# Hybrid encoder on one core: the output projection's weight sums paced by the local strips, and a v strip at the end of chunk 2

## The chip, the core and the metric

The kernel runs on one core of one Trainium2 chip. The metric is device time in microseconds (us) of one execution. Five engines work side by side: TensorE (PE in the profile, its weight loads PEld), VectorE (DVE), ScalarE (ACT), GpSimd (POOL) and SyncE (SP), which here issues every DMA. Each engine has its own instruction stream, worked through in order; semaphores tie the streams together. Sixteen DMA engines carry the transfers.

## The reference

One encoder layer is applied to a prompt of 1024 tokens and to a sample of 256 tokens, each with 16 meta tokens in front, model width 2048, float32:

```python
u = rms_norm(h, norm_w) @ w_in
qa, ka, va, za, qb, kb, vb, zb = jnp.split(u, split_points(), axis=-1)
qa = rope(rms_norm(qa, q_norm_a)); ka = rope(rms_norm(ka, k_norm_a))
ya = global_gqa(qa, ka, va) * jax.nn.silu(za)             # 8 heads, 2 key/value heads
qb = rms_norm(qb, q_norm_b); kb = rms_norm(kb, k_norm_b)
yb = neighbourhood_attention(qb, kb, vb, rpb) * jax.nn.silu(zb)  # 8 heads, windows of 8 x 16
y = jnp.concatenate([ya, yb], axis=-1) @ w_out
return h + y
```

A head is 128 wide. The input projection has 52 column strips of 128: for the global heads 8 q, 2 k, 2 v and 8 z, for the local heads 8 each of q, k, v and z.

## The kernel before

**Precision.** A float32 product is made of three matmuls in a reduced format. Each operand is split into a high part (a cast on ScalarE) and the remainder (a subtraction on VectorE); `split`, L48, does both.

**Two chunks.** Tokens are worked in two chunks: `chunk1` (L456) has the meta tokens, the sample and 384 prompt tokens (656 columns), `chunk2` (L564) the other 640. In each chunk x is loaded tile by tile into the pool `xr` (four buffers, L962), scaled, split and kept for the whole chunk (`get_x`, L72). Then the strips follow.

**A strip.** `strips` (L104) multiplies one 128-wide column strip of `w_in` with the chunk's tokens: sixteen 128 x 128 tiles in four pieces of 256 KB, 96 matmuls into two PSUM tiles of pool `pp` (four buffers). The pieces are loaded into `raw` and split into `w` (four buffers each), traced at a higher priority (`woff`) so that they run ahead. In chunk 1 the low part is also stored to `wld`, and chunk 2 loads it back. `project` (L424) calls `strips` and then evacuates: q and k with an RMS norm (`qk_evac`, L136; a partition sum on GpSimd, for global heads the rope with four small DMAs `ts` per block), v with a product and transposes on TensorE (`v_rows`, `v_turn`), z with a silu made of Abs, Exp, Ln and Exp on ScalarE (`z_evac`, L176). The first `project` call of a chunk does two strips together (k and v), as does the last one of chunk 1 (v and z).

**Order of strips.** Chunk 1 runs 20 global strips (k, v, and per head z and q, each head followed by a small attention over two key tiles, `attend`) and then 32 local strips (k, q, v, z per head, each head followed by `attend_sample`). Chunk 2 runs the global strips with four attention blocks per head. Its local strips are in the list `late` (L713); eight of them are put between the global heads (`fill`), the others alternate with blocks of the local attention of heads 0 to 6 (`local_blocks`, L703). `v_local` (L604) stores v to `vn`, and `v_windows` loads the windows from there; `z_late` stores z to `zd`, and `z_load` loads it. The four blocks of the last local head run among the first eight products of the output projection.

**Weight sums.** The output projection (`outproj`, L869) uses seven products of half-size blocks instead of eight, which needs differences of the blocks of `w_out`. `w_sums` (L434) makes them ahead of time: a generator of sixteen steps, and a step loads four pieces of 256 KB into `xr` (tile `wq`), does four subtractions on VectorE (L439) and stores four pieces to `td`. `project` advances it at every second strip once more than 8 have been traced.

**Output projection.** At its start the PSUM pool `pp` is closed and `pq` opens in its place; the y halves (`yr`, in the buffers of `xr`) are loaded, combined and split into `ym`, which lies where chunk 2's x was. `products` (L815) does 48 matmuls a step.

**What sets the order.** The kernel's text gives a priority by order of tracing. A scheduler simulates the machine as the program is built and, for each engine, takes the ready instruction that was traced first; an instruction that is ready early runs early, unless a buffer, a dependence or an explicit order holds it back. `issue_after(i)` gives such an order: what is traced in it on i's engine is queued behind i, without a wait for i's end.

Of the kernel before, what the change touches and what calls it, by code (L numbers as in the profile page):

```python
# [12 lines left out]
F32 = mybir.dt.float32  # L13
F32R = mybir.dt.float32r
AF = mybir.ActivationFunctionType
ALU = mybir.AluOpType
# [24 lines left out]
QA, KA, VA, ZA, QB_, KB, VB, ZB = 0, 8, 10, 12, 20, 28, 36, 44  # L41


class Kern:
# [3 lines left out]
    def split(self, hi, lo, full):  # L48
        nc = self.nc
        nc.scalar.copy(hi, full)  # L50
        nc.vector.tensor_tensor(out=lo, in0=full, in1=hi.bitcast(F32), op=ALU.subtract)  # L51

    def rsqrt(self, ms, n):

# [49 lines left out]
    def strips(self, jobs, getx):  # L104


        nc, tc = self.nc, self.tc
        out = [[pool.tile([P, 512], F32, tag=tag, name="pp") for pool, tag in pools] for _, _, pools in jobs]
        for c in range(KT // WCH):
            ws = []  # L110
            for s, _, _ in jobs:
                with tc.high_priority(offset=self.woff):
                    w = self.raw.tile([P, WCH, P], F32, tag="raw", name="wr")
                    self.lastw = nc.sync.dma_start(w[:], self.io["w_in"][s][:, c * WCH:(c + 1) * WCH, :]).ins
                    wh = self.w.tile([P, WCH, P], F32R, tag="wh", name="wh")
                    wl = self.w.tile([P, WCH, P], F32R, tag="wl", name="wl")
                    if self.second:
                        nc.sync.dma_start(wl[:].bitcast(F32), self.wld[s][:, c * WCH:(c + 1) * WCH, :])
                        nc.scalar.copy(wh[:], w[:])  # L119
                    else:  # L120
                        self.split(wh[:], wl[:], w[:])
                ws.append((wh, wl))
                if not self.second:
                    nc.sync.dma_start(self.wld[s][:, c * WCH:(c + 1) * WCH, :], wl[:].bitcast(F32))
            for k in range(WCH):
                kt = c * WCH + k
                xh, xl = getx(kt)
                for (wh, wl), ps, (_, blocks, _) in zip(ws, out, jobs):
                    for p, (o, n) in zip(ps, blocks):
                        first, last = kt == 0, kt == KT - 1  # L130
                        nc.tensor.matmul(p[:, :n], wh[:, k, :], xh[:, o:o + n], start=first, stop=False)  # L131
                        nc.tensor.matmul(p[:, :n], wh[:, k, :], xl[:, o:o + n], start=False, stop=False)  # L132
                        nc.tensor.matmul(p[:, :n], wl[:, k, :], xh[:, o:o + n], start=False, stop=last)  # L133
        return out
# [289 lines left out]
    def project(self, *parts):  # L424

        if not self.second:
            self.projected += len(parts)
            if self.projected > 8 and self.projected % 2 == 0:
                next(self.sums, None)
        jobs = [(p[0], p[1], [p[3] if len(p) > 3 else (self.pp, "pp")] * len(p[1])) for p in parts]  # L430
        out = self.strips(jobs, self.get_x)
        return [p[2](ps) for p, ps in zip(parts, out)]

    def w_sums(self):  # L434

        nc, w = self.nc, self.io["w_out"]

        def sub(out, a, b):
            nc.vector.tensor_tensor(out=out, in0=a, in1=b, op=ALU.subtract)  # L439

        for s in range(8):
            for i in range(0, 8, WCH):
                q = {}
                for n, c, j in (("12", 8 + s, i), ("11", s, i), ("22", 8 + s, 8 + i), ("21", s, 8 + i)):
                    r = self.xr.tile([P, WCH, P], F32, tag="xr", name="wq")
                    nc.sync.dma_start(r[:], w[c][:, j:j + WCH, :])
                    q[n] = r[:]
                sub(q["11"], q["12"], q["11"])
                sub(q["12"], q["22"], q["12"])
                sub(q["22"], q["22"], q["11"])  # L450
                sub(q["21"], q["22"], q["21"])
                for n, p in (("11", 5), ("12", 7), ("22", 6), ("21", 4)):
                    nc.sync.dma_start(self.td[s][p][:, i:i + WCH, :], q[n])
                yield
# [109 lines left out]
    def chunk2(self):  # L564
        nc, io = self.nc, self.io
# [38 lines left out]
        def v_local(s, h):  # L604

            def evac(ps):
                for p, (o, n) in zip(ps, BL):
                    j, e = 3 + o // P, 3 + (o + n) // P
                    vt = self.ev.tile([P, n // P, P], F32, tag="ev", name="vl")
                    nc.scalar.copy(vt[:], self.v_turn(self.v_rows(p, o, n), range(0, n, P)))  # L610
                    nc.sync.dma_start(self.vn[h][P * j:P * e].rearrange("(t p) d -> p t d", p=P), vt[:])
            return s, BL, evac
# [12 lines left out]
        def q_strip(s, h, wc, rope):  # L625
            q = self.q.tile([P, 2, NP], F32R, tag="q", name="q")
            nc.sync.dma_start(q[:, :, :C1P].bitcast(F32), self.qd[h][:])

            def evac(ps):
                for p, (o, n) in zip(ps, BL):  # L630
                    rp = (ct[:, o:o + n], st[:, o:o + n]) if rope else None
                    self.qk_evac(p, o, n, wc, rp, [(0, n, q[:, 0, C1P + o:C1P + o + n], q[:, 1, C1P + o:C1P + o + n])])
                return q
            return s, BL, evac
# [12 lines left out]
        def qk_late(s, wc, dst):  # L647
            def evac(ps):
                for p, (o, n) in zip(ps, BL):
                    self.qk_evac(p, o, n, wc, None, [(0, n, dst[:, o:o + n], None)])  # L650
            return s, BL, evac

        def z_late(s, dst):
            def evac(ps):
                for p, (o, n) in zip(ps, BL):
                    zt = self.ev.tile([P, n], F32, tag="ev", name="zt")
                    self.z_evac(p, o, n, [(0, n, zt[:])])
                    nc.sync.dma_start(dst[:, C1P + o:C1P + o + n], zt[:])
            return s, BL, evac
# [53 lines left out]
        late = []  # L713
        for h in range(NH):
            late += [qk_late(KB + h, kwb, self.k2d[2 + h]), qk_late(QB_ + h, qwb, self.q2d[8 + h]),
                     v_local(VB + h, h), z_late(ZB + h, self.zd[8 + h])]

        def fill(n):
            for _ in range(min(n, len(late))):
# [2 lines left out]
        for g in range(2):  # L722
# [5 lines left out]
            for h in range(4 * g, 4 * g + 4):  # L728
                z, = pr(z_strip(ZA + h, h) + (((self.sp, "sp"),) if h == 0 else ()))
                q, = pr(q_strip(QA + h, h, qw, True))  # L730
# [327 lines left out]
```

## Time and profile before

| | |
|---|---|
| median of 3 runs | 2307.06 us (2305.71 to 2307.85) |
| the profiled execution | 2303.17 us, span 2301.4 us |
| PE, PEld busy | 2233.8 us (97%), 2218.7 us (96%) |
| DVE, ACT, POOL busy | 1594.2 us (69%), 1145.0 us (50%), 525.1 us (23%) |
| DMA | 424.54 MB, mean 184 GB/s |
| loads `wq` and stores `td` | 64 each, 256 KB, 5.9 and 4.4 us to landing (median) |
| mean granted clock of TensorE | 0.991 |

The page is of one execution. Times in the trace count from the span's start. A group's row has the line, the engine, the operation, output and inputs by the program's names, the shape and the count, then busy time, the mean of one in ns, and the engine's idle time before the instructions with what ended it. Rows of waits read: who waited, for what, us in total, how often, the longest. "SPq" is SP's queue issuing a DMA.

### The profile page before, as it was taken

To read this page: it belongs to the slowest core of one execution; us is meant where nothing else is said; L and a number is where in the kernel's file an instruction comes from. 1 tells how busy PE (TensorE), PEld (TensorE's weight loads), DVE (VectorE), ACT (ScalarE), POOL (GpSimd) and SP (SyncE) were. 2 spreads that over 40 slices of the span, in tenths; PEclk is the share of its full clock that TensorE was granted. 3 is DMA by queue.
4 is the path that set the end of the run, shared out by engine and by line. 5 is a ranking of instruction groups with operands and counts; after the bars stand their busy time and mean duration, and the time that the engine had idled before them with its cause. 6 is when DMAs were issued, how large, how long until landed. Compare 5 with 4: busy or idle time off the path is not lost.

```text
span 2301.4 us, 42253 instructions
## 1 busy us (share of the span) xinstructions
PE 2233.8 (97%) x15550; PEld 2218.7 (96%) x15550; DVE 1594.2 (69%) x2988; ACT 1145.0 (50%) x2432; POOL 525.1 (23%) x275
## 2 busy tenths in 40 slices
PE   7988999999999999999999999999999989999999
PEld 6888889999999999999999999999999989999999
DVE  5787578555555565999988999887665667545753
ACT  5444345444344456677767667655444454232220
POOL 0232033112212112342323322333333222000000
PEclk9999999999999999999999999999999999999999
DMA  7888886555555567444544444477777764755663
GB/s 237 258 273 258 283 268 191 179 168 173 175 172 173 172 205 214 120 125 133 135 137 130 128 130 125 150 206 221 212 207 214 209 194 115 231 177 171 184 206 116
DMA packets 279856, 424.54 MB, mean 184 GB/s; under 512 B 48576, under 2 KB 121184, under 8 KB 279648
## 3 DMA queue, kind: packets, MB, share of 16 engines
q1 hardware_dynamic: 279648, 421.84, 60.6%
q8 instruction: 122, 2.00, 0.4%
q14 instruction: 86, 0.70, 0.1%
HBM read 296.25 MB, written 118.90 MB: 180 GB/s over the span
## 4 chain that ended last, share of the span: by engine, by line
PE 79%; DMA 11%; DVE 5%; ACT 2%; SPq 2%; issue 1%; POOL 1%; DVEq 0%; POOLq 0%; ACTq 0%
PE pp L132 17%; PE pp L133 16%; PE pp L131 16%; PE pq L826 5%; PE pq L825 5%; PE pq L824 5%; DMA wq<-in_w_out 3%; DMA xr<-in_x 2%; DMA td<-wq 1%; PE sp L253 1%; PE po L295 1%; PE po L294 1%; PE po L293 1%; PE sp L254 1%; PE sp L255 1%
## 5 line engine op out<-in xcount | busy, mean ns | idle before, releaser
L131 PE MATMUL pp<-xh,wh 128*128 128x384 f32 (+2 forms) x3328 | 1030.6, 313 | 21.7 <-ACT xh L81 17.5
L132 PE MATMUL pp<-xl,wh 128*128 128x384 f32 (+2 forms) x3328 | 1037.1, 312 | 0.5 <-DVE xl L82 0.2
L133 PE MATMUL pp<-xh,wl 128*128 128x384 f32 (+2 forms) x3328 | 1037.6, 312 | 0.0
L131 PEld LDWEIGHTS pp<-xh,wh 128*128 128x128 f32 x3328 | 628.5, 190 | 24.8 <-ACT xh L81 19.8
L132 PEld LDWEIGHTS pp<-xl,wh 128*128 128x128 f32 x3328 | 630.7, 190 | 2.1 <-DVE xl L82 2.1
L133 PEld LDWEIGHTS pp<-xh,wl 128*128 128x128 f32 x3328 | 630.8, 190 | 0.1
L51 DVE TENSOR_TENSOR wl<-wr,wh 128x512 fp32r<-128x512 f32 x320 | 238.7, 759 | 155.1 <-ACT wh L50 130.5
L141 POOL PARTITION_ALL_REDUCE m<-ms x104 | 234.5, 2254 | 410.7 <-ACT ms L139 304.0
L824 PE MATMUL pq<-ym,wh 128*128 128x320 f32 x896 | 277.7, 310 | 8.9 <-DVE z L179 8.9
L826 PE MATMUL pq<-ym,wl 128*128 128x320 f32 x896 | 277.9, 310 | 0.0
L825 PE MATMUL pq<-ym,wh 128*128 128x320 f32 x896 | 277.6, 310 | 0.0
L50 ACT CAST wh<-wr 128x512 fp32r<-128x512 f32 x320 | 193.2, 617 | 161.6 <-PE pp L132 104.0
L222 POOL PARTITION_ALL_REDUCE tot<-a x80 | 170.2, 2128 | 437.2 <-DVE a L220 425.7
L205 POOL PARTITION_ALL_REDUCE ma<-m x80 | 113.4, 1418 | 494.5 <-DVE m L203 494.5
L824 PEld LDWEIGHTS pq<-ym,wh 128*128 128x128 f32 x896 | 169.0, 189 | 9.1 <-ACT ym L50 9.1
L825 PEld LDWEIGHTS pq<-ym,wh 128*128 128x128 f32 x896 | 169.0, 189 | 0.0
L826 PEld LDWEIGHTS pq<-ym,wl 128*128 128x128 f32 x896 | 169.0, 189 | 0.0
L119 ACT CAST wh<-wr 128x512 fp32r<-128x512 f32 x208 | 127.7, 615 | 55.2 <-PE pp L132 52.6
L57 ACT ACTIVATE rs_l<-m 128x384 f32<-128x384 f32 (+2 forms) x104 | 49.1, 472 | 141.1 <-DVE m L142 141.0
L51 DVE TENSOR_TENSOR pl<-S,ph 128x512 fp32r<-128x512 f32 x136 | 95.9, 711 | 7.9 <-ACT ph L50 7.8
L257 ACT COPY S<-sp 128x512 f32<-128x512 f32 x136 | 78.1, 580 | 45.6 <-PE sp L255 38.5
L274 ACT ACTIVATE S<-S 128x512 f32<-128x512 f32 x136 | 83.9, 629 | 32.0 <-DVE S L273 31.8
(200 smaller groups left out, 3396.2 us busy)
## 6 DMA issues: line engine op xcount, KB each, us to landing
wr<-in_w_in SPq DMA_DIRECT2D x416, 256.0 KB, 3.7
wld<-wl SPq DMA_DIRECT2D x208, 256.0 KB, 3.8
wl<-wld SPq DMA_DIRECT2D x208, 256.0 KB, 3.4
yr<-yd SPq DMA_DIRECT2D x72, 320.0 KB, 4.0
wq<-in_w_out SPq DMA_DIRECT2D x64, 256.0 KB, 5.9
td<-wq SPq DMA_DIRECT2D x64, 256.0 KB, 4.4
wr<-td SPq DMA_DIRECT2D x64, 256.0 KB, 3.5
wr<-in_w_out SPq DMA_DIRECT2D x48, 256.0 KB, 4.0
```

Source lines behind the costliest of these rows:

```text
L50: nc.scalar.copy(hi, full)
L51: nc.vector.tensor_tensor(out=lo, in0=full, in1=hi.bitcast(F32), op=ALU.subtract)
L119: nc.scalar.copy(wh[:], w[:])
L131: nc.tensor.matmul(p[:, :n], wh[:, k, :], xh[:, o:o + n], start=first, stop=False)
L132: nc.tensor.matmul(p[:, :n], wh[:, k, :], xl[:, o:o + n], start=False, stop=False)
L133: nc.tensor.matmul(p[:, :n], wl[:, k, :], xh[:, o:o + n], start=False, stop=last)
L141: nc.gpsimd.partition_all_reduce(m2[:], ms[:], P, RED.add)
L205: nc.gpsimd.partition_all_reduce(ma[:], m1[:], P, RED.max)
L222: nc.gpsimd.partition_all_reduce(tot[:], a1[:], P, RED.add)
L824: nc.tensor.matmul(ps[:, b, :B], wh, yh[:, o], start=k == 0, stop=False)
L825: nc.tensor.matmul(ps[:, b, :B], wh, yl[:, o], start=False, stop=False)
L826: nc.tensor.matmul(ps[:, b, :B], wl, yh[:, o], start=False, stop=k == 7)
```

## The change

`w_sums` now yields twice a step: after its four loads, and after the subtractions and stores. The subtractions are put behind the last weight split traced so far, which `split` now returns and `strips` keeps as `lastsplit`. `project` advances the generator at each call once more than 18 strips have been traced: the first loads are traced at strip 19, the first subtractions at strip 20, the last ones at strip 50. In chunk 2, each local head's z strip is now ahead of its v strip, so the last strip before the output projection is a v strip.

```diff
@@ split
-        nc.vector.tensor_tensor(out=lo, in0=full, in1=hi.bitcast(F32), op=ALU.subtract)
+        return nc.vector.tensor_tensor(out=lo, in0=full, in1=hi.bitcast(F32), op=ALU.subtract).ins
@@ strips
-                        self.split(wh[:], wl[:], w[:])
+                        self.lastsplit = self.split(wh[:], wl[:], w[:])
@@ project
-            if self.projected > 8 and self.projected % 2 == 0:
+            if self.projected > 18:
                 next(self.sums, None)
@@ w_sums
                     q[n] = r[:]
-                sub(q["11"], q["12"], q["11"])
-                sub(q["12"], q["22"], q["12"])
-                sub(q["22"], q["22"], q["11"])
-                sub(q["21"], q["22"], q["21"])
+                yield
+
+                with self.tc.issue_after(self.lastsplit):
+                    sub(q["11"], q["12"], q["11"])
+                    sub(q["12"], q["22"], q["12"])
+                    sub(q["22"], q["22"], q["11"])
+                    sub(q["21"], q["22"], q["21"])
                 for n, p in (("11", 5), ("12", 7), ("22", 6), ("21", 4)):
                     nc.sync.dma_start(self.td[s][p][:, i:i + WCH, :], q[n])
                 yield
@@ chunk2
-                     v_local(VB + h, h), z_late(ZB + h, self.zd[8 + h])]
+                     z_late(ZB + h, self.zd[8 + h]), v_local(VB + h, h)]
```

## The prediction

> **What bounds the kernel now.** I first read the forty slices of the page and the lines of its chain.
>
> ```profile
> PE   7988999999999999999999999999999989999999
> ...
> DMA  7888886555555567444544444477777764755663
> ...
> PE pp L132 17%; PE pp L133 16%; PE pp L131 16%; PE pq L826 5%; PE pq L825 5%; PE pq L824 5%; DMA wq<-in_w_out 3%; DMA xr<-in_x 2%; DMA td<-wq 1%; PE sp L253 1%; PE po L295 1%; PE po L294 1%; PE po L293 1%; PE sp L254 1%; PE sp L255 1%
> ```
>
> TensorE is the bound nearly everywhere. It is short of full in the first slices (57.5 us each) and in slice 33, and the first six slices are also the ones where the DMA engines are fullest. The chain names two transfers of the weight sums, the loads `wq` and the stores `td`. So I asked when the sums run.
>
> ```profile
> L446 SPq DMA_DIRECT2D wq<-in_w_out x64: 328/424/1242, 49.2 to 330.8; - x64
> L439 DVE TENSOR_TENSOR wq<-wq x64: 669/692/1630, 55.4 to 337.2; 128x512 f32<-128x512 f32 x64
> L453 SPq DMA_DIRECT2D td<-wq x64: 319/327/726, 56.1 to 343.5; - x64
> ...
> DMA to landing us min/median/max: 2.0/5.2/8.6
> ```
>
> All sixteen steps run between 49 and 344 us, though the text traces them over strips 10 to 40: nothing but a free `xr` buffer holds their loads back. That is the stage of the 20 global strips with rope. Next, busy time by stretch (columns: us, PE, PEld, DVE, ACT, POOL, granted clock, DMA share, GB/s).
>
> ```profile
> 56.00:350.00 294.00, 264.64 (x1701) 256.98 (x1700) 211.91 (x402) 130.93 (x295) 72.98 (x31) 0.95 0.85 265
> 240.00:270.00 30.00, 30.00 (x208) 30.00 (x207) 12.52 (x23) 9.85 (x22) 2.10 (x2) 1.00 0.91 296
> 360.00:840.00 480.00, 480.00 (x3296) 479.83 (x3295) 266.51 (x479) 203.65 (x441) 101.96 (x51) 1.00 0.57 174
> ...
> 890.00:1330.00 440.00, 439.67 (x3225) 438.99 (x3224) 387.76 (x750) 307.54 (x671) 142.71 (x68) 1.00 0.47 132
> ```
>
> From 360 to 840 us (local strips of chunk 1) TensorE never stops: 480.00 / 3296 = 145.6 ns a matmul. At that pace the 1701 matmuls of 56 to 350 us need 247.7 us, and they took 294. The **excess is 46.3 us**: 29.4 of idle time and 16.9 of slower busy time, to which the granted clock of 0.95 answers (0.05 x 294 = 14.7). The clock falls after idle gaps, for example:
>
> ```profile
> 170.69 0.38 PE L253 MATMUL sp<-qs,kc 128*128 128x256 f32 x1 [2.90 <-ACT qs L50]
> ```
> ```profile
> 66.30:69.70 3.40, 3.40 (x17) 3.40 (x17) 1.96 (x4) 1.42 (x3) 1.00 (x1) 0.50 1.11 286
> ...
> 172.10:175.50 3.40, 3.40 (x16) 3.37 (x15) 1.38 (x3) 1.79 (x4) 0.00 (x0) 0.51 0.92 229
> ```
>
> What TensorE waits for between 56 and 350 us, and then what VectorE waits for from 50 to 350 us:
>
> ```profile
> PE sp L253 <- ACT qs L50: 10.9, 6, 4.9
> PE po L293 <- ACT ph L50: 8.6, 5, 3.7
> PE pp L131 <- ACT t L145: 4.1, 3, 1.9
> PE po L296 <- DVE Pm L215: 3.8, 3, 2.3
> PE po L295 <- DVE pl L51: 1.3, 1, 1.3
> ```
> ```profile
> DVE wq L439 <- DMA wq<-in_w_out: 46.3, 22, 5.9
> DVE t L150 <- DMA ts<-t: 12.7, 12, 2.1
> ```
>
> TensorE waits for operands of the small attentions (q's split, the probabilities) and for PSUM that the rope copy `t` frees. Each comes through VectorE, and VectorE, which works in order, stands 46.3 us (that this equals the excess is chance) before subtractions whose loads have not landed. No wait of TensorE there is for a weight split.
>
> **The change part by part.** *1. The sums leave the rope stage.* Now a step takes two calls: four loads, then, one strip later, four subtractions queued on VectorE behind the last weight split traced, and four stores. The first subtractions are traced at strip 20, the last at strip 50 of 52. Only the subtractions carry an order, but the next step's loads need the four `xr` buffers that this step's stores free, so all but the first four loads follow. Out of the stage go 64 x 0.692 = 44 us of VectorE, its waits of 46.3, 64 x (0.424 + 0.327) = 48 us of issuing on SP's queue (where the rope transfers `ts` stand behind them) and 128 x 256 KB = 33.6 MB. The gain is bounded below by 0 (if the attentions' latencies alone make the gaps) and above by 46.3. The nearest row is chunk 2's own stage with rope and attention, free of sums: 439.67 of 440 us busy, at a clock of 1.00, although VectorE is at 0.88 there. So most goes. I leave standing the three start-up waits for `t` (4.1), half a clock over one 3.4 us period (1.7), and 4 for the other waits, since chunk 1's attention has two key tiles and less work to fill in: 10 stay, **36.3 are gained**.
>
> A rule of the Trainium skill bears on what remains: "TensorE: Matmul & The Clock Gate", Part 1, says that the clock halves after an idle window of about 3.4 us. The row above shows a half clock after a gap of 2.90 us, so I go by the row. By the rule short gaps would cost their idle time alone, and some 2 us less would stay.
>
> *2. The sums enter the local stage of chunk 1.* Fifteen of the sixteen steps, 31.5 MB over 480 us, add 66 GB/s to 174: 240 GB/s, share 0.57 x 240 / 174 = 0.79. VectorE gets 41.5 us, (266.5 + 41.5) / 480 = 0.64. The loads land in 5.2 us and are issued about a step (two strips of 96 matmuls, 28 us) before their subtraction, so VectorE should not wait; behind a subtraction that does wait stand the next splits and the evacuations. SP gets 45 us of issuing, past weight loads made strips ahead. Lower bound 0: the 240 to 270 us row has TensorE full at a DMA share of 0.91. Upper bound: each step costs what it costs today, 46.3 / 16 = 2.9 us, 43 for fifteen. I take **+1**, near the row.
>
> *3. The change of chunks.* Chunk 2's x loads use the same four buffers. Their first issue is
>
> ```profile
> 837.94 0.33 SPq L77 DMA_DIRECT2D xr<-in_x  x1
> ```
>
> The last subtractions follow strip 49's last split, which is made while strip 48 ends, four strips (56 us) before the end of chunk 1; the stores are down by then. **0**; without that cover, a load and a store landing of some 5 us each stand before the first x.
>
> *4. v last in chunk 2.* No instruction is added; per local head v's two evacuations, five transposes and stores change place with z's. Only the end shows it (PE, then DVE):
>
> ```profile
> 1885.87 0.61 PE L824 MATMUL pq<-ym,wh 128*128 128x320 f32 x1 [8.93 <-DVE z L179]
> ...
> 1892.95 0.28 PE L389 MATMUL po<-Pm,vm 128*128 128x256 f32 x1
> ```
> ```profile
> 1875.01 0.56 DVE L179 TENSOR_TENSOR z<-pp,rb 128x384 f32<-128x384 f32 x1 [1.32 <-PE pp L133]
> ...
> 1883.78 0.82 DVE L51 TENSOR_TENSOR ym<-yr,ym 128x640 fp32r<-128x640 f32 x1 [2.30 <-ACT ym L50]
> ...
> 1885.32 0.41 DVE L179 TENSOR_TENSOR z<-pp,rb 128x256 f32<-128x256 f32 x1
> ...
> 1889.42 0.81 DVE L51 TENSOR_TENSOR ym<-yr,ym 128x640 fp32r<-128x640 f32 x1
> ```
>
> The first product waits 8.93 us for PSUM that z's second read holds; that read stands on VectorE behind a y operand waiting for its load. v's read has no chain of ScalarE functions before its second block, so it should stand earlier. What is late next is the eighth y operand, ready at 1890.2: with six matmuls the product then ends at 1891.1, where now 38 of its 48 matmuls are issued by 1892.95 and the end is near 1894.4 (ten more at 145.6 ns). The gain is at most 3.3. A loss: the second v read may stand just as late, with its transposes then in front of the products; call it 5. The stored v must also come back:
>
> ```profile
> vw<-vn SPq DMA_DIRECT2D x32, 256.0 KB, 4.4
> ...
> vn<-vl SPq DMA_DIRECT2D x8, 128.0 KB, 3.2
> ```
> ```profile
> 1912.94 0.39 PE po L389
> ```
>
> From a store near 1880 that is 1888, and the last head's first block uses it after 1912.94: hidden. I take **-2**, nearer to the gain, since the read now in the way is z's own.
>
> *Sum.* The profiled execution took 2303.17 us (span 2301.4): 2303.2 - 36.3 + 1 - 2 = 2265.9. It lies 3.9 below the median of 2307.06, so against the runs shown I forecast **2270**.
>
> **Rivals.** *A, half the gaps are the attention's own.* For: `ts` waits of 12.7 us have nothing to do with the sums' loads as such, and two key tiles leave little to fill with. Against: chunk 2's row. Then 23 are gained: 2307 - 23 + 1 - 2 = 2283.
> *B, slower: the loss moves along.* Place: VectorE's queue among the local strips. If a step's loads come late there as they do now, it stands before the subtraction and the splits behind it run out; price 2.9 us a step, 43 in all: 2307 - 36.3 + 43.4 - 2 = 2312. It decides from 38.3 / 15 = 2.55 us a step. Against: loads two strips ahead, and no weight split among TensorE's waits even now.
> *C, the end goes wrong.* Part 4 costs 5 instead of gaining 2: 2277.
> *D, the change does not do what it says.* The subtractions might still run early, as no load has an order: 2307. Against: the order on VectorE is explicit, and stores and buffers hang on it.
>
> **How the numbers follow.** Chances: forecast 0.58 (own range 2262 to 2280, 3 to 18 us staying), A 0.22, C 0.06, B 0.10, D 0.04. The range runs from all 46.3 and 3.3 gained (2258) to A with some more lost in part 2 (2298), and leaves out B and D, 0.14. A measurement here tells 0.2% (4.6 us) from nothing: faster 0.86 (forecast, A, C); slower 0.08 (most of B); same 0.06 (D and the rest of B).
>
> **What would show it.** In the changed profile the `wq` subtractions start near 300 us and end near 790, in sixteen bunches 28 us apart; VectorE's wait for `wq` falls from 46.3 us to under 5; the rope stage ends some 36 us earlier with a clock near 1.00; the local stage is still full, with about 240 GB/s; the wait at L824 is under 6 us and names no z. The forecast is wrong if waits for `qs` and `ph` keep their 19.5 us without the sums (A), or if TensorE shows gaps in the local stage (B).

## The result and the profile after

The changed kernel takes **2249.36 us** (median of 4 runs, 2246.17 to 2249.59), the kernel before 2306.43 us in the same comparison. The ratio is 0.9749, 95% interval 0.9732 to 0.9766: 57 us faster. I had forecast 2270 us and a range from 2258 to 2298. The sign and the two places were right, the size was not: the time lies below the whole range.

The slices, and TensorE's waits of the whole span, of the changed kernel:

```profile
PE   7999999999999999999999999999999999999999
...
DMA  7656578777777775444454344476767664845663
```
```profile
PE pp L131 <- ACT xh L81: 16.9, 8, 7.9
PE pq L827 <- DVE vt L166: 1.3, 1, 1.3
...
PE sp L253 <- ACT qs L50: 0.9, 1, 0.9
```

After the first slice TensorE is full, and the DMA row has moved: lower in slices 2 to 6, higher in 7 to 15. What is left is mostly the wait for x when a chunk starts. The stretches that answer to those of before (same columns: us, PE, PEld, DVE, ACT, POOL, clock, DMA share, GB/s):

```profile
56.00:306.00 250.00, 248.67 (x1709) 247.56 (x1708) 182.29 (x344) 131.54 (x297) 63.35 (x31) 1.00 0.61 186
...
310.00:750.00 440.00, 440.00 (x3025) 439.01 (x3024) 278.95 (x502) 187.05 (x410) 95.24 (x45) 1.00 0.78 245
```

The rope stage's 1700 matmuls now fit into 250 us at a clock of 1.00, where they took 294 us at 0.95. The local stage carries the sums' bytes (245 GB/s instead of 174) without a gap. By the starts of the strips on TensorE the changed kernel is 44.2 us ahead at the last global strip of chunk 1 (351.3 before, 307.1 after), still 43 us ahead at the last strip of chunk 2, and 53.8 us ahead at the end of the span. So the tail gives 11 us more. There, the first matmul of the output projection, and then the rows of the sums' loads and subtractions:

```profile
1835.11 0.39 PE L827 MATMUL pq<-ym,wh 128*128 128x320 f32 x1 [1.29 <-DVE vt L166]
```
```profile
L446 SPq DMA_DIRECT2D wq<-in_w_out x64: 327/333/863, 50.2 to 728.0; - x64
L439 DVE TENSOR_TENSOR wq<-wq x64: 676/683/694, 293.7 to 750.3; 128x512 f32<-128x512 f32 x64
```

The wait of 8.93 us before that matmul is now 1.29 us. The subtractions run from 294 to 750 us, and VectorE no longer has any wait for `wq`.

### The profile page after: what moved, and what is told of

Same layout as the page of the kernel before. It is cut to its first block, busy times and chain, and to the rows that moved or that the text cites. A ratio compares the mean times of both kernels' runs of the same rounds, so it can differ in the third digit from the quotient of the medians.

```text
span 2247.6 us, 42246 instructions
## 1 busy us (share of the span) xinstructions
PE 2218.2 (99%) x15550; PEld 2208.7 (98%) x15550; DVE 1596.4 (71%) x2988; ACT 1141.5 (51%) x2432; POOL 526.5 (23%) x275
## 4 chain that ended last, share of the span: by engine, by line
PE 90%; DVE 4%; DMA 3%; ACT 1%; POOL 1%; issue 1%; SPq 0%; DVEq 0%; POOLq 0%; ACTq 0%
PE pp L132 20%; PE pp L133 20%; PE pp L131 20%; PE pq L827 6%; PE pq L829 6%; PE pq L828 6%; DMA xr<-in_x 2%; PE po L392 1%; PE po L295 1%; PE po L293 1%; PE po L294 1%; PE sp L253 1%; PE sp L254 1%; PE sp L255 1%; DVE S L273 1%
## 5 line engine op out<-in xcount | busy, mean ns | idle before, releaser
L131 PEld LDWEIGHTS pp<-xh,wh 128*128 128x128 f32 x3328 | 625.7, 189 | 19.5 <-ACT xh L81 19.2
L61 DVE TENSOR_TENSOR rs_l<-m,rs_l 128x384 f32<-128x384 f32 (+2 forms) x104 | 75.4, 725 | 33.6 <-ACT rs_l L60 33.5
```

## Experiments

Ratios are to the kernel before, which took 2305 to 2308 us in every comparison.

### The two parts alone

The first kernel has only the sums' part of the change, the second only the order of the late strips ("v last": in each local head of chunk 2, z ahead of v).

```diff
 # sums_only: the changed kernel, but
-                     z_late(ZB + h, self.zd[8 + h]), v_local(VB + h, h)]
+                     v_local(VB + h, h), z_late(ZB + h, self.zd[8 + h])]
 # v_last_only: the kernel before, but
-                     v_local(VB + h, h), z_late(ZB + h, self.zd[8 + h])]
+                     z_late(ZB + h, self.zd[8 + h]), v_local(VB + h, h)]
```

> The weight sums as in the changed kernel, the local heads of chunk 2 in the old order (z last). By strip starts the changed kernel is 44.2 us ahead at the end of the rope stage, 42.9 us ahead at the last strips of chunk 2 and 53.8 us ahead at the end of the span, so the sums alone should be worth 43 to 44 us and the rest, 11 us, should be the end's. Theory 'two independent parts': about 2263 us, with the wait of about 9 us for z's read (L179) still before the first product. Rival 'the end gains from the sums too' (its operands ready earlier because chunk 2 runs in another rhythm): about 2252 us, without that wait.

> The kernel before with the local heads of chunk 2 in the new order (v last), the sums as before. Theory 'two independent parts': 2306.4 - 10.8 = 2296 us, the wait before the first product about 1.3 us, the products of the first two steps interleaved. Rival 'the end gains from the sums too': 2304 to 2306 us. My forecast had 2 us for this part.

With the sums alone: 2258.35 us, ratio 0.9791 (0.9776 to 0.9806), 47.8 us faster. With v last alone: 2295.95 us, ratio 0.9952 (0.9936 to 0.9969), 10.2 us faster. Together 58, against 57 for the whole change: the parts add. TensorE's longest wait in the kernel with the sums alone, and in the one with v last alone (from 1800 us on):

```profile
PE pq L827 <- DVE z L179: 8.3, 1, 8.3
```
```profile
PE pq L824 <- DVE vt L166: 1.3, 1, 1.3
```

### The order on VectorE

```diff
-                with self.tc.issue_after(self.lastsplit):
-                    sub(q["11"], q["12"], q["11"])   # and the three others
+                sub(q["11"], q["12"], q["11"])       # and the three others
```

> The changed kernel without the order of the subtractions behind the last weight split: the two calls a step, strip 19 as the start and v last stay. Theory 'the order carries the change': all steps run between 50 and 345 us again, VectorE waits about 46 us for wq, and only the end's gain stays, about 2296 us. Rival 'the later tracing is enough': 2249 us, sums from 290 us on.

The time is 2295.49 us, ratio 0.9951 (0.9935 to 0.9966): what v last alone gives. VectorE's wait for the sums is back (50 to 350 us):

```profile
DVE wq L439 <- DMA wq<-in_w_out: 41.6, 20, 7.8
```

In the order of instructions on VectorE, the first step stands after 11 weight splits, as in the kernel before, and after 76 in the changed one. Tracing the steps later does nothing by itself; the one explicit order carries the sums' part.

### Is it VectorE's wait?

My reason for the loss was that VectorE, in order, stands before subtractions whose loads are late. The next kernel brings those waits into the local stage.

```diff
+                    self.lastlow = nc.sync.dma_start(self.wld[s]...).ins       # in strips
...
-            if self.projected > 18:
+            if self.projected > 18 and self.projected % 2 == 0:
...
-                    nc.sync.dma_start(r[:], w[c][:, j:j + WCH, :])
+                    with self.tc.issue_after(self.lastlow):
+                        nc.sync.dma_start(r[:], w[c][:, j:j + WCH, :])
...
-                yield                                   # between loads and subtractions
```

> As the changed kernel (sums in the local strips of chunk 1, v last), but a step is one call at every second strip, and its four loads are queued on SP behind the store of the last weight split's low part, so that the subtractions stand close behind their own loads as in the kernel before. Theory W, 'waiting does it' (VectorE standing before subtractions whose loads have not landed holds up everything behind it): VectorE waits 30 to 45 us for wq, and the loss travels along, 2265 to 2290 us. Theory S, 'the stage does it' (the rope stage has short slack, the local stage has much): VectorE waits as long, TensorE keeps 480 of 480 us in the local stage, 2249 to 2252 us.

The time is 2266.38 us, ratio 0.9831 (0.9814 to 0.9848): 17 us slower than the changed kernel, 40 us faster than before. Between 310 and 800 us VectorE waits as long as it did in the rope stage, and TensorE, which lost nothing there in the changed kernel, is no longer full in the local stage:

```profile
DVE wq L439 <- DMA wq<-in_w_out: 47.8, 18, 4.3
```
```profile
360.00:790.00 430.00, 421.67 (x2879) 418.11 (x2878) 256.50 (x459) 170.14 (x373) 82.18 (x41) 1.00 0.78 239
```

So such waits do cost something, here about 17 / 16 = 1.1 us a step, but nothing like the 2.9 us a step of the rope stage with the same wait. Two kernels then keep the sums in the rope stage, one step at each strip from the third on, two calls a step. The first has the four `xr` buffers; in the second every other step loads into the buffer of chunk 2's q, so that loads go out a strip ahead.

```diff
 # rope_stage: the changed kernel, but
-            if self.projected > 18:
-                next(self.sums, None)
+            if self.projected > 2:
+                for _ in range(1 if self.projected == 3 else 2):
+                    next(self.sums, None)
 # rope_ahead: that, and in w_sums
+                odd = self.q.tile([P, 4, WCH, P], F32, tag="q", name="wodd") if i else None
-                    r = self.xr.tile([P, WCH, P], F32, tag="xr", name="wq")
+                    r = odd[:, len(q)] if i else self.xr.tile([P, WCH, P], F32, tag="xr", name="wq")
```

> The changed kernel (two calls a step, subtractions behind the last weight split, v last), but with one step at every strip from the third on, so that all sixteen steps stay in the rope stage and end with it. With four buffers a step's loads still wait for the stores of the step before, so they land close to their subtractions. The same transfers and subtractions in the same stage as in the kernel before. Theory W (waits of VectorE for late loads make the loss): VectorE still waits 20 to 40 us for wq and about as large a part of the 44 us stays lost, 2270 to 2290 us. Theory T (the extra traffic and issuing in the rope stage make the loss, whoever waits): 2290 to 2296 us.

> As the rope-stage kernel, but every second step loads into an SBUF buffer that chunk 1 does not use (that of chunk 2's q), so that there are eight buffers and a step's loads are issued a strip or more ahead of its subtractions. Theory W: VectorE's wait for wq falls under 10 us and most of the loss goes although the sums stay in the rope stage, 2250 to 2262 us. Theory T: as the rope-stage kernel within 5 us, 2285 to 2296 us.

Rope stage: 2282.19 us, ratio 0.9897 (0.9882 to 0.9912). Rope ahead: 2286.71 us, ratio 0.9912 (0.9897 to 0.9927). Both have v last, so they compare with 2295.95 us: 14 and 9 us less than with the sums in the old place. VectorE's longest waits in the two (50 to 350 us), and of the second TensorE's longest wait and its stretch:

```profile
DVE wq L440 <- DMA wq<-in_w_out: 22.8, 9, 6.1
DVE t L150 <- DMA ts<-t: 15.2, 9, 2.8
```
```profile
DVE t L150 <- DMA ts<-t: 38.9, 13, 9.3
```
```profile
PE sp L253 <- ACT qs L50: 20.7, 6, 6.2
```
```profile
56.00:340.00 284.00, 257.93 (x1695) 254.83 (x1694) 210.02 (x394) 129.96 (x292) 75.32 (x31) 0.96 0.87 275
```

**My theory falls here.** In the second kernel VectorE waits only 2.8 us for the sums, and its last global strip still starts 38.8 us later than in the changed kernel (44.2 in the kernel before). It is even slower than the first, which waits eight times as long for `wq`. When the sums' loads are out of the way, another wait grows: for `ts`, the rope's small transfers, up to 9.3 us at a time; and TensorE waits for q's split, which comes behind them. What remains to choose from is the queue of SP, VectorE's extra work, and the bytes.

### Queue, work or bytes

Three kernels issue `ts` from ScalarE instead of SP; one leaves the subtractions out.

```diff
 # before_ts_act, rope_ahead_ts_act, after_ts_act
-                nc.sync.dma_start(ts[32 * i:32 * i + 32], t[...])
+                nc.scalar.dma_start(ts[32 * i:32 * i + 32], t[...])
 # rope_ahead_no_sub: rope_ahead without the four sub(...), the stores paced by
+                    with self.tc.issue_after(self.lastlow):
                         nc.sync.dma_start(self.td[s][p][:, i:i + WCH, :], q[n])
```

> The kernel before, with the rope's four small transfers ts issued by ScalarE, which has just made their source, and no longer by SP. The sums stay where they were. Theory Q (SP's one queue: ts stands behind the sums' loads, stores and their waits, so the rope's operands are late and with them the attention): half or more of the 44 us comes back, 2262 to 2284 us. Theory B (the DMA engines themselves, at a share of 0.85, make everything land late): ts lands as late as before, 2300 to 2308 us. Theory W (VectorE before late sums) predicts no gain either, 2300 to 2308 us, since VectorE's wait for wq stays near 46 us.

> The rope-ahead kernel (sums in the rope stage, loads a strip ahead, VectorE's wait for wq 2.8 us, its wait for ts 38.9 us) with ts issued by ScalarE. Theory Q: the wait for ts falls under 15 us and the kernel comes to 2250 to 2262 us. Theory B: 2280 to 2288 us.

> The changed kernel with ts issued by ScalarE. TensorE is full there already (no gap over 0.9 us in the rope stage), so all theories say 2248 to 2251 us; it is the control for the issue cost on ScalarE, and a candidate for a better version.

> The rope-ahead kernel without the 64 subtractions: the loaded blocks go to td as they are, so the output projection works on wrong weight sums; loads, stores and their order against the strips stay. It takes 44 us of work from VectorE in the rope stage. Theories Q and B: the loss stays, 2278 to 2288 us. Theory V (VectorE's extra work makes the rope's chain late): most of it goes, 2250 to 2265 us.

| kernel | us | ratio (95%) |
|---|---|---|
| before, ts on ScalarE | 2302.06 | 0.9978 (0.9968 to 0.9987) |
| rope ahead, ts on ScalarE | 2289.57 | 0.9928 (0.9912 to 0.9945) |
| changed, ts on ScalarE | 2259.39 | 0.9795 (0.9781 to 0.9810) |
| rope ahead, no subtractions | 2281.55 | 0.9889 (0.9869 to 0.9909) |

Moving `ts` past SP's queue brings 5 us in the kernel before, nothing in the rope-ahead kernel, and costs 10 in the changed one, where I had expected no change. The next table shows the way of `ts`. It is worked out from the instructions in order of time, as a mean over the 20 rope blocks of chunk 1, in us from the end of the copy `t` to the landing of the last of its four transfers:

```
                        to the first issue   four issues   last issue to landing   total
changed                        0.80             2.80              1.85              5.45
before                         2.23             3.12              1.94              7.29
before, ts on ScalarE          0.95            4.74              3.44              9.13
rope stage                     2.21            2.90              2.42              7.52
rope ahead                     3.64            3.12              2.48              9.25
rope ahead, no subtractions    4.04            3.03              2.05              9.12
rope ahead, ts on ScalarE      0.67             5.12              3.22              9.01
changed, ts on ScalarE         0.26             3.81              3.15              7.22
quarter bytes                  1.57             2.85              1.94              6.36
quarter issues                 0.82             2.86              2.03              5.71
```

On ScalarE the first issue is prompt, but the four issues and the landing take longer; only in the rope-ahead kernel is the way a little shorter. This test therefore does not clear SP's queue by itself. Nor does the way of `ts` rank the kernels: the kernel before with `ts` on ScalarE has a longer one and is 5 us faster, and the changed kernel with `ts` on ScalarE has as long a one as the kernel before and takes 48 us less, 10 of them by v last. (Of the 8.0 us that the profiled execution of that kernel is behind the changed one, 3.5 are lost by the last global strip and 3.9 more among the local strips, which have no rope; why is not shown.) Without 44 us of VectorE's work the rope-ahead kernel gains 5 us: the work is not the main cause either. The last two kernels cut the bytes with the same number of issues, and both bytes and issues.

```diff
 # both, from rope_ahead: the output projection reads w_out where it read td
-        ...get(p, lambda: self.td[s][p][:])()
+        ...get(p, lambda: self.io["w_out"][8 + s][:, :8, :])()
 # quarter_bytes: 128 transfers of 64 KB
-                    nc.sync.dma_start(r if i else r[:], w[c][:, j:j + WCH, :])
+                    r = (r if i else r[:])[:, :1]
+                    nc.sync.dma_start(r, w[c][:, j:j + 1, :])
-                    nc.sync.dma_start(self.td[s][p][:, i:i + WCH, :], q[n])
+                    nc.sync.dma_start(self.td[s][p][:, i:i + 1, :], q[n])
 # quarter_issues: 32 transfers of 256 KB
-                for n, c, j in (("12", 8 + s, i), ("11", s, i), ("22", 8 + s, 8 + i), ("21", s, 8 + i)):
+                for n, c, j in (("12", 8 + s, i),):
```

> The rope-ahead kernel with each of the sums' 128 transfers cut from 256 to 64 KB and each subtraction to a quarter of its width; the output projection reads blocks of w_out where it would read the sums. Same number of issues on SP in the rope stage, a quarter of the bytes. Theory B (the DMA engines at a share of 0.87 make the rope's small transfers and all else late): most of the loss goes, 2250 to 2258 us. Theory Q (SP's queue, 128 issues and their waits ahead of ts): the loss stays, 2275 to 2287 us.

> The same quarter of the bytes and of the subtractions as in the quarter-bytes kernel, in 32 transfers of 256 KB in place of 128 of 64 KB. Theory B: as the quarter-bytes kernel within 4 us. Theory Q: 20 to 30 us faster than the quarter-bytes kernel, 2250 to 2258 us.

Quarter bytes: 2254.04 us, ratio 0.9780 (0.9765 to 0.9794). Quarter issues: 2253.66 us, ratio 0.9782 (0.9766 to 0.9798). The stretch of the first, and its wait for `ts` (50 to 350 us):

```profile
56.00:340.00 284.00, 279.68 (x1913) 277.69 (x1912) 213.45 (x449) 147.41 (x335) 74.74 (x35) 1.00 0.70 210
```
```profile
DVE t L150 <- DMA ts<-t: 18.6, 13, 4.2
```

With all 128 issues still on SP and three quarters of the bytes gone, the time falls from 2286.71 to 2254.04; dropping 96 issues as well changes nothing. **In this kernel it is the bytes.** At a DMA share of 0.87 the rope's path is late and the last global strip starts 38.8 us later than in the changed kernel, whose share is 0.61 (56 to 306 us); at 0.70 it starts 3.6 us later, and the whole kernel is within 5 us of the changed one. About 5 of these 33 us may be the subtractions, which were cut too; that is what the kernel without them gained. The kernel before has the same bytes in the same stage, but no run cuts them in its order. SP's queue plays a part all the same, as the place where it shows: the first issue of `ts` comes after 3.64 us with all the bytes and after 1.57 us with a quarter of them, at the same number of issues.

### The end

```diff
 # z_reads_first: sums_only, and in z_late both L179 products ahead of the first block's chain
+                zs = [self.z_read(p, o, n) for p, (o, n) in zip(ps, BL)]
-                for p, (o, n) in zip(ps, BL):
+                for p, (o, n), z in zip(ps, BL, zs):
...
-                    self.z_evac(p, o, n, [(0, n, zt[:])])
+                    self.z_evac(p, o, n, [(0, n, zt[:])], z)
```

> The sums as in the changed kernel, z last as in the kernel before, but the late z strips read both PSUM blocks (L179) before the first block's chain of ScalarE functions. Theory P (the end's loss is the second PSUM read of the last strip, standing on VectorE behind a y operand whose load is late): the wait before the first product falls from 8.3 to under 2.5 us, 2249 to 2251 us, as with v last. Rival (the z strip's functions on ScalarE and its store hold the end, wherever the read stands): 2257 to 2259 us, as with the sums alone.

The time is 2254.04 us (2250.58 to 2257.02), ratio 0.9775 (0.9758 to 0.9791). The wait for z is gone, with z still the last strip; from 1800 us on TensorE waits:

```profile
PE sp L362 <- DVE S L369: 2.8, 1, 2.8
PE pq L833 <- DVE ym L51: 1.4, 1, 1.4
```

The median lies between the sums alone (2258.35) and the changed kernel (2249.36). The profile bears out that the place of the second PSUM read makes the 8.3 us wait. The profiled execution, the fastest of the four at 2250.58 us, has the new wait of 2.8 us and is 1.2 us behind the changed kernel's (2249.38); what makes the other three slower is not shown.

## Why the prediction was right and wrong

**What failed.** I forecast 36.3 - 1 = 35.3 us for the sums; alone they bring 47.8 by medians, 12.5 more. I forecast 2 us for v last; alone it brings 10.2, 8.2 more. Together these are the 20.6 us between 2270 and 2249.36. The range failed mainly by the second term: its fast end allowed 46.3 us for the sums and 3.3 for v last, and v last passed its bound by 6.9 us, the sums theirs by 1.5.

**Part 1, the sums leave the rope stage: right in place and sign, under-sized, and its mechanism wrong.** The excess of 46.3 us was read correctly from the pace of the local stage: it was all there to gain. The failing step is the 10 us left standing. Nothing stayed: the three start-up waits for `t` (4.1 us) were no property of the start-up but part of the same loss, and with the gaps the half clock went too. The row that I had named as the nearest, chunk 2's rope stage at 439.67 of 440 us, was the right guide, and I marked it down by an argument (two key tiles, little to fill with) that no row supported.

The reason I gave, VectorE standing 46.3 us before late loads, is not needed for the loss: with that wait at 2.8 us, 38.8 of the 44.2 us by strip starts were still lost, and in the local stage a wait of 47.8 us costs 17 us. In the rope-ahead kernel the bytes are the cause: 33.6 MB more in a stage that without them moves 186 GB/s bring the DMA share to 0.87, and this stage's chain from q to its scores goes through the DMA engines. For the kernel before, with the same bytes in the stage and a share of 0.85, this is argued and not shown, and the path there may be another. Of TensorE's waits, 13.7 of 29 us there are for `ph`, `Pm` and `pl`, and the way from the scores to these has no transfer on it; VectorE's stand before late loads can be how the bytes act there. Its wait of 12.7 us for `ts` proves nothing: the changed kernel, with TensorE full, has 14.9 us. The sums' move had to help under either reason, since it takes the bytes and the waits out of the stage together. That the sign came out right is therefore luck as far as my reason goes.

I had the share of 0.85, and read 0.91 at 240 to 270 us with TensorE full as proof that a high share does no harm. But in that window TensorE ran strips and three transposes and no attention, and VectorE was busy 12.5 of 30 us. The window showed that weight loads survive a high share, which is what the local stage needs, and not that the rope's chain does.

**Part 2, the sums enter the local stage: right.** Taken at +1; the stretch shows 440.00 of 440 us, 245 GB/s against my 240 and a share of 0.78 against 0.79. Rival B named the right condition: with loads that are not ahead a part of the loss does travel, 1.1 us a step instead of the 2.9 I priced.

**Part 3, the change of chunks: right in its 0, with a row misread.** The load at 837.94 us that I took for chunk 2's first x load is the fourth. The first three go out as soon as the sums leave the buffers: at 338 to 350 us in the kernel before, at 751.5 to 755.7 in the changed one, behind the last subtraction at 750. They land by 760.7, and x is first used at 791.9, so the delay costs nothing; TensorE's wait at the change of chunks is 2.59 us (2.77 before).

**Part 4, v last: right in sign, wrong in its bound.** I took -2 and allowed a gain of at most 3.3, "what is late next is the eighth y operand". It gave 10.2 us. The failing step is that bound. The y operands are as late as I said (the eighth is ready 14.9 us after the last strip's end in the kernel before, 15.5 in the changed one), but TensorE does not wait for them: the scheduler sets the matmuls of the second product, on the other PSUM tile, between those of the first. In the program order of TensorE the kernel before has 48 matmuls of one tile and then the next tile's; the changed one has 13, 9, 11, 4 and so on in turn. The profile shows it by the copies that empty the two tiles (ScalarE, `u`): 1899.87 and 1909.81 before, 1851.01 and 1853.93 after. An earlier read of the strip's PSUM is enough for it: with z read first the copies stand at 1851.97 and 1852.54, where the sums alone have 1855.85 and 1866.31. In the kernel before, the wait was followed by a stretch at half clock:

```profile
1878.80:1889.00 10.20, 3.13 (x12) 3.16 (x13) 7.87 (x17) 6.95 (x15) 1.23 (x1) 0.50 0.98 358
```

Counted up, as an estimate: the wait falls by 8.93 - 1.29 = 7.6 us; TensorE's 3.13 us of work in that stretch now go at full clock, some 1.6 us; and a wait of 1.68 us before the last head's first block (its `Pm`, at L389) is gone: 10.9 us.

**Rivals.** A (half the gaps are the attention's own) fell: the waits for `qs` and `ph` went from 19.5 us to 0.9. C fell. D did not happen, but the kernel without the order shows that it was one line away.

**The clock.** The wait for x at the start of chunk 2 in the changed kernel lasts 2.59 us, and a half clock follows. The same wait in the kernel before lasts 2.77 us, and the clock stays full:

```profile
835.29 0.74 PE L131 MATMUL pp<-xh,wh 128*128 128x384 f32 x3 [2.59 <-ACT xh L81]
```
```profile
836.00:839.40 3.40, 3.22 (x13) 3.19 (x13) 2.73 (x5) 3.09 (x6) 0.00 (x0) 0.50 0.94 313
```
```profile
879.73 0.74 PE L131 MATMUL pp<-xh,wh 128*128 128x384 f32 x3 [2.77 <-ACT xh L81]
```
```profile
879.70:884.00 4.30, 4.09 (x26) 3.83 (x27) 3.61 (x5) 3.98 (x7) 0.00 (x0) 1.00 0.84 286
```

The Trainium skill ("TensorE: Matmul & The Clock Gate", Part 1) asks for an idle window of about 3.4 us; here 2.59 us was enough once and 2.77 us was not. So a gap of this size can bring a half-clock stretch with it, and its length alone does not tell whether it will.

## What to carry to other kernels

Put background transfers where TensorE waits for no chain of work that goes through the DMA engines, and look at the DMA share of the stage that they leave as much as at that of the stage they enter. The longest wait of an engine in a stage need not be the cause of the stage's loss: take the wait away and see whether the time follows. Before calling a late operand the next bound, look for other work that the scheduler can set in front of it.

## What the runs showed of the hardware

Four `ts` transfers issued from ScalarE took longer than from SP, 3.81 against 2.80 us for the four issues in the changed kernel, and landed 1.3 us later after the last issue (3.15 against 1.85): there a second issuing engine did not shorten the way. And the loss was steep in the bytes: in the same stage TensorE waited 1.4 us in all at a DMA share of 0.61, and against that the last global strip came 3.6 us later at 0.70 and 38.8 us later at 0.87. The share alone does not fix the loss: the rope-stage kernel, at 0.88, was 34.0 us late, the kernel before, at 0.85, 44.2 us. Why the first issue on SP itself comes later with more bytes at the same number of issues was not settled.
